# Gate tables of two expert blocks written by accumulating indirect DMAs in place of one-hot products

## The chip, the core and the metric

The kernel runs on one core of a Trainium2 chip. The metric is the device time of one execution in microseconds, from the first to the last instruction of the program with what little lies around it. The engines are named as the profile names them: PE (TensorE: matrix products, and PEld its weight loads), DVE (VectorE), ACT (ScalarE), POOL (GpSimd, which here only issues indirect DMAs), SP (SyncE, which issues every other DMA). Each engine works through its own instructions strictly in order; the engines wait for each other and for DMAs through semaphores.

## What is computed

One decoder layer on 1024 tokens of width 1024, all in float32: an attention branch and an mLSTM branch, merged by gates (the "front" below), and then a PEER expert layer on the result. The expert layer is the part that the change touches. Cut to what matters:

```python
q = (xb @ w_query).reshape(t, 8, 2, 64)                     # 8 heads, 2 halves
s = einsum('thpd,hpkd->thpk', q, sub_keys)                  # 128 keys for each half
top_s, top_i = top_k(s, 16)
cand_s = top_s[:, :, 0, :, None] + top_s[:, :, 1, None, :]  # 16 x 16 pairs
best_s, best_pos = top_k(cand_s, 16)                        # 16 experts of 16384, for each head
gate = softmax(best_s)
act = gelu(einsum('td,thkd->thk', xb, expert_down[idx]))
out = einsum('thk,thkd->td', gate * act, expert_up[idx])
```

So each token has 8 x 16 = 128 chosen experts, each with a gate. An expert's number is a pair (i, j) of two key numbers below 128. Two heads of a token may choose the same expert; its gates then add.

## The kernel before

The 1024 tokens are 8 blocks of 128, in 4 groups of two blocks. `front` runs once for each group: projections (`wpart` loads a piece of a weight strip, L209; for most strips it is split into a high part `whi` by ACT, L214, and a low part `wlo` by DVE, L215, and PE multiplies three times, L231 to L233; the later strips are multiplied unsplit, L229), attention, mLSTM, merging, the query product, and the scores `sc`, which go to HBM.

The expert layer is done in two ways. Blocks 0, 6 and 7 are "sparse": `down` gathers, for each of the 128 choices, one row of 4 KB for each token from HBM by an indirect DMA on POOL (`fetch`, L743), and DVE forms the product of that row with the token (L756, a product with a sum, followed by a short read of the sum); `up` gathers the second table in the same way and accumulates (L770). Blocks 1 to 5 are "dense": `dense` runs over all 16384 experts, 128 at a time in `hidden` (L809: PE products; then ACT's gelu and DVE's product with the gates, L816) and sums in `outputs` (L830 to L834). For this a dense block's gates are needed as a full table [expert][token], mostly zeros, in HBM (`gate_d`).

`topk` (DVE for the most part) finds the choices of a block while the next group's front runs. For a dense block, `spread` then makes the table by one-hot products: for each token DVE builds two matrices, `oi` (row i holds the gate, L727) and `oj` (column j holds a one, L730, a fourth of them on ACT), and PE multiplies them (L735), which puts each gate into the cell (i, j) and adds where two fall into one. Four tokens are a "quad": 4 products, one copy by ACT into `stage` (L736); four quads fill one `stage` of 1 MB, which SP writes to `gate_d` (L738). A dense block has 32 quads, five blocks have 160. The front asks for them by `fill`, 3 quads for 4 calls, within the gate and output projections of the following group: block 1 in group 1's front, blocks 2 and 3 in group 2's, blocks 4 and 5 in group 3's.

Block 0's `down` is done during the front. Its 128 products each stand behind one matmul of the front (`pace`: a dependence without a semaphore, on places from 0.4 to 0.95 of the front's list of matmuls), and its gathers use two buffers `g` (pool `gather`): gather n can be issued when product n-2 is done. Blocks 6 and 7's `down` and the `up` of all three run during `dense`, with five buffers.

The order of instructions on each engine is set by the Tile scheduler, from priorities (as a rule the order in which the code is written; `later` puts the `topk` of a group 5000 steps later) and from its own estimate of when operands are ready. Indirect DMAs of POOL share eight semaphores, so each waits for the one eight before it.

Of the kernel before, what the change touches and what calls it, by code (L numbers as in the profile page):

```python
# [10 lines left out]

F32 = mybir.dt.float32
F32R = mybir.dt.float32r
I32 = mybir.dt.int32
U32 = mybir.dt.uint32
AF = mybir.ActivationFunctionType
ALU = mybir.AluOpType
AX = mybir.AxisListType
PSUM = bass.MemoryType.PSUM
NOSYNC = mybir.DependencyInfo(mybir.DependencyClass.NoSync, mybir.DependencyReason.DATA)  # L20

P = 128
S = 1024
# [10 lines left out]
TMAX = P * max(len(g) for g in GROUPS)  # L34
SPARSE = (0, 6, 7)
DENSE = (1, 2, 3, 4, 5)
ND = P * len(DENSE)
GT = 16
GJ = 4
EG = 4  # L40
LATER = 5000
QUADS = 0.75
PACE0, PACE1 = 0.4, 0.95
WB = 4
PD0, PD1 = 0.06, 0.98

# [8 lines left out]
def layout(inputs):  # L55
    w = np.asarray(inputs["w_in"])[0]
    cols = [w[:, :1024], w[:, 1280:3328], w[:, 3344:6416],
            np.asarray(inputs["w_branch_attn"])[0], np.asarray(inputs["w_branch_mlstm"])[0],
            np.asarray(inputs["w_out"])[0], np.asarray(inputs["peer_w_query"])[0],
            w[:, 1024:1280]]  # L60
    a = {}
    a["x"] = np.asarray(inputs["x"])[0]
    a["pos"] = np.asarray(inputs["positions"])[0].reshape(NB, P).T
    a["wmain"] = np.concatenate([strips(c) for c in cols], axis=0)
    a["wif"] = w[:, 3328:3344].reshape(NC, P, 16).transpose(1, 0, 2)
    col = lambda v: np.asarray(v)[0].reshape(NC, P).T
# [18 lines left out]
    a["iota"] = np.arange(P, dtype=np.float32)[None]  # L85
    return {k: np.ascontiguousarray(v) for k, v in a.items()}


def build(nc, tc, a, out, dbg=None):
# [5 lines left out]
    dp = pool("dram", 1, outer, space=bass.MemoryType.DRAM)  # L95
    kp = pool("topk", 2)
    ks = pool("spread", 1)
    gp = pool("gather", 2)
    st = pool("state", 1)
    wp = pool("weights", 1)  # L100
    fp = pool("front", 1)
# [29 lines left out]
    gains = const("gains", [P, 3, NC], pool=st)  # L131
    x_first = []
    pos = const("pos", [P, NB], dt=I32, pool=st)
    freq = bcast("freq", 8, st)
    qkg = bcast("qkg", 128, st)
    wifr = t4([P, NC, 16], "wifr")
# [54 lines left out]
    xb_d = dp.tile([NB, P, D], F32, name="xb_d")  # L191
    xbT_d = dp.tile([len(DENSE), P, NC, P], F32, name="xbT_d")
    sc_d = dp.tile([NB, 2, P, 8, P], F32, name="sc_d")
    gate_d = dp.tile([P, P // GJ, ND // GT, GJ, GT], F32, name="gate_d")

    RING = 3
    kT = st.tile([P, 2, RING, P], F32, name="kT")
# [9 lines left out]
    def wpart(i, q, split):  # L207
        t = wp.tile([P, 4, 256], F32, name="w", bufs=WB)
        SY.dma_start(t, a["wmain"][i, :, 4 * q:4 * q + 4, :])  # L209
        if not split:  # L210
            return t, None
        hi = wp.tile([P, 4, 256], F32R, name="whi", bufs=3)
        lo = wp.tile([P, 4, 256], F32R, name="wlo", bufs=3)
        A.copy(hi, t)  # L214
        V.tensor_tensor(lo, t, hi.bitcast(F32), ALU.subtract)  # L215
        return hi, lo
# [430 lines left out]
    def topk(b):  # L647
# [15 lines left out]
        for qh in range(4):  # L663
# [23 lines left out]
            for p, n in ((0, 17), (1, 16)):  # L687
# [4 lines left out]
                V.tensor_tensor(eqh, eqh, tif[:, :, p, None, 0:n].to_broadcast([P, 2, 16, n]), ALU.mult)  # L692
                V.tensor_reduce(ef[:, p, cols], eq, AX.X, ALU.add)
        gate = (bp.tile([P, 8, 16], F32, name="gate", bufs=len(SPARSE)) if b in SPARSE
                else ks.tile([P, 8, 16], F32, name="dgate", bufs=2))
# [7 lines left out]
        if b in SPARSE or dbg:  # L703
# [1 line left out]
            V.scalar_tensor_tensor(idx, ef[:, 1], 128.0, ef[:, 0], ALU.mult, ALU.add)  # L705
            probe("idx", idx, b)
            probe("gate", gate, b)
        if b in DENSE:
            r["spread"] = spread(ef, gate, DENSE.index(b))
        return r  # L710

    def spread(ef, gate, k):
# [3 lines left out]
            T.transpose(ps[:, n, :], src, ident)  # L716
        A.copy(cols, ps[:, 0:3, :])
        for c in range(P // GT):
            stage = ks.tile([P, P, GT], F32, name="stage", bufs=2)
            for q in range(GT // 4):  # L720
                ps = pat.tile([P, 4, P], F32, name="at")
                for u in range(2):
# [15 lines left out]
                    SY.dma_start(gate_d[:, :, k * (P // GT) + c], stage.rearrange("p (n g) t -> p n g t", g=GJ))  # L738
                yield

    def fetch(p, table, idx, s):
        t = p.tile([P, D], F32, name="g")
        G.indirect_dma_start(out=t, out_offset=None, in_=a[table],  # L743
                             in_offset=bass.IndirectOffsetOnAxis(ap=idx[:, s:s + 1], axis=0))
        return t

    def down(r, b, pace, p):
        act = bp.tile([P, P], F32, name="act", bufs=1)
        xb = bp.tile([P, D], F32, name="xb", bufs=1)
        SY.dma_start(xb, xb_d[b])  # L750
        gain = p.tile([P, D], F32, name="g")
        SY.dma_start(gain, a["gain2"].to_broadcast([P, D]))
        V.tensor_tensor(xb, xb, gain, ALU.mult)
        for s in range(P):
            t = fetch(p, "down", r["idx"], s)
            ins = V.tensor_tensor_reduce(out=t, in0=t, in1=xb, scale=1.0, scalar=0.0, op0=ALU.mult,  # L756
                                         op1=ALU.add, accum_out=act[:, s:s + 1])
            after(ins, next(pace, None))
        coef = bp.tile([P, P], F32, name="coef")
        A.activation(coef, act, AF.Gelu)  # L760
        V.tensor_tensor(coef, coef, r["gate"].rearrange("p h k -> p (h k)"), ALU.mult)
        r["coef"] = coef

    def up(r, b, pace, p):
        acc = p.tile([P, D], F32, name="acc", bufs=1)
# [8 lines left out]
    def dense():  # L774
# [26 lines left out]
        def hidden(j, g):  # L801
# [10 lines left out]
                    mark("dense", ins)  # L812
            act = tp.tile([P, ND], F32, name="act", bufs=1)
            A.activation(act.rearrange("p (u t) -> p u t", u=NH), ps[:, :, 0:W], AF.Gelu)
            av_ = act.rearrange("p (c t) -> p c t", t=GT)
            V.tensor_tensor(av_, av_, g, ALU.mult)  # L816
# [20 lines left out]

        work = []
        for n in range(P // EG):
            g = tp.tile([P, ND // GT, GJ, GT], F32, name="g")  # L840
            SY.dma_start(g, gate_d[:, n])
            new = []
            for e in range(EG):
                new.append(hidden(EG * n + e, g[:, :, e, :]))
# [19 lines left out]
    res = {}  # L864
# [14 lines left out]
            pass  # L879
    later(GROUPS[-1])  # L880
    names = anchors["front"]
    names = names[int(PACE0 * len(names)):int(PACE1 * len(names))]
    pace = iter([names[i * len(names) // P] for i in range(P)])
    down(res[0], 0, pace, gp)
    inner.close()
    gd = dense()
    names = anchors["dense"]
# [19 lines left out]
```

## Time and profile before

| | us |
|---|---|
| median of 3 timed runs | 3559.62 (3559.30 to 3559.77) |
| the profiled execution | 3545.12 |
| its span, first to last instruction | 3543.4 |
| first product of `dense` (L809) | 1734.9 |
| first and last one-hot product (L735) | 593.4, 1682.8 |
| first and last product of block 0's `down` | 646, 1599 |

The span has two parts: the front with everything that runs beside it (up to 1734.9 us), and `dense` (1734.9 us to the end). The groups' fronts begin to load anew at about 14, 366, 775 and 1249 us (every fiftieth `wlo`). "Busy" of an engine is time in which it has an instruction; "idle before" stands with what ended the idle time. The granted clock is TensorE's share of full speed.

### The profile page before, as it was taken

The numbers are of one execution on the slowest core, as the hardware profiler recorded it, in microseconds if no ns is written. First come the engines' busy times: TensorE is split into PE (matmuls) and PEld (weight loads), VectorE is DVE, ScalarE is ACT, GpSimd is POOL, SyncE is SP. The second block draws the span as 40 slices with busy tenths as digits, with TensorE's granted clock in tenths as the row PEclk, the third lists the DMA queues.
The fourth block names the chain that finished last, engine by engine and source line by source line (L and its number), as shares of the span: only waits on it lengthen the run. The fifth ranks groups of instructions, "written<-read, shape, count | busy, mean of one in ns | idle before, by whom it ended". The sixth has DMA issues, their size and how long they took to land.

```text
span 3543.4 us, 55473 instructions
## 1 busy us (share of the span) xinstructions
PE 3378.6 (95%) x20579; PEld 3044.3 (86%) x20579; DVE 2743.1 (77%) x6406; ACT 1363.0 (38%) x2730; POOL 985.7 (28%) x772
## 2 busy tenths in 40 slices
PE   7999999999998789989799999999999999999999
PEld 7898988888887678887688898999989999898998
DVE  5332689739898468988598988888888888889985
ACT  6652567338574346635322222222222222222221
POOL 0000000110001221110004654545455455545542
PEclk9999999999999888999899999999999999999999
DMA  4344434874378874686727988889888888888884
GB/s 149 108 143 166 164 115 145 256 261 141 117 212 252 274 247 150 206 244 174 252 101 276 329 307 321 321 284 329 285 315 305 294 321 299 312 308 302 325 288 160
DMA packets 386670, 846.66 MB, mean 239 GB/s; under 512 B 189280, under 2 KB 195168, under 8 KB 382304
## 3 DMA queue, kind: packets, MB, share of 16 engines
q1 hardware_dynamic: 275808, 440.42, 37.7%
q0 software_dynamic: 110592, 402.70, 32.5%
q8 instruction: 162, 2.65, 0.3%
q14 instruction: 108, 0.88, 0.1%
HBM read 780.11 MB, written 62.91 MB: 238 GB/s over the span
## 4 chain that ended last, share of the span: by engine, by line
PE 66%; DVE 13%; issue 8%; DMA 7%; POOL 3%; ACT 3%; SPq 0%; POOLq 0%; DVEq 0%; ACTq 0%
PE ph L809 19%; PE pj L229 8%; PE po L830 6%; PE po L833 6%; PE po L834 6%; PE pj L231 4%; PE pj L233 4%; PE pj L232 4%; DMA g<-down,idx 3%; POOL g L743 3%; DVE oi L727 2%; PE at L735 2%; DMA w<-wmain 1%; DVE g L756 1%; DMA g<-up,idx 1%
## 5 line engine op out<-in xcount | busy, mean ns | idle before, releaser
L743 POOL DMA_INDIRECT g<-down,idx x384 | 480.2, 1250 | 1769.3 <-DVE act L756 879.2
L743 POOL DMA_INDIRECT g<-up,idx x384 | 505.3, 1316 | 732.8 <-DVE acc L770 373.9
L756 DVE CUSTOM_DVE_ANT_0 g<-g,xb 128x1024 f32<-128x1024 f32 x384 | 462.6, 1219 | 167.2 <-DMA g<-down,idx 166.6
L770 DVE SCALAR_TENSOR_TENSOR acc<-g,coef,acc 128x1024 f32<-128x1024 f32 x384 | 491.7, 1281 | 46.8 <-DMA g<-up,idx 36.8
L830 PE MATMUL po<-hu,ah 128*128 128x512 f32 x1280 | 499.2, 390 | 2.3 <-DVE y L836 2.3
L809 PE MATMUL ph<-xbh,hd 128*128 128x320 f32 x2048 | 470.6, 311 | 31.7 <-ACT hd L797 22.8
L833 PE MATMUL po<-lu,ah 128*128 128x512 f32 x1280 | 498.5, 389 | 0.0
L834 PE MATMUL po<-hu,al 128*128 128x512 f32 x1280 | 498.1, 389 | 0.0
L809 PE MATMUL ph<-xbh,ld 128*128 128x320 f32 x2048 | 470.5, 311 | 5.3 <-DVE ld L798 5.3
L809 PE MATMUL ph<-xbl,hd 128*128 128x320 f32 x2048 | 469.9, 311 | 0.0
L797 ACT CAST hu<-rawu 128x1024 fp32r<-128x1024 f32 x128 | 131.5, 1051 | 738.9 <-PE po L834 557.0
L809 PEld LDWEIGHTS ph<-xbh,hd 128*128 128x128 f32 x2048 | 346.6, 189 | 35.3 <-ACT hd L797 23.2
L215 DVE TENSOR_TENSOR wlo<-w,whi 128x1024 fp32r<-128x1024 f32 x200 | 243.3, 1218 | 142.1 <-ACT whi L214 142.0
L809 PEld LDWEIGHTS ph<-xbh,ld 128*128 128x128 f32 x2048 | 345.1, 189 | 7.0 <-DVE ld L798 6.7
L809 PEld LDWEIGHTS ph<-xbl,hd 128*128 128x128 f32 x2048 | 345.6, 189 | 0.0
L214 ACT CAST whi<-w 128x1024 fp32r<-128x1024 f32 x200 | 209.3, 1047 | 235.9 <-DMA w<-wmain 100.1
L836 DVE TENSOR_TENSOR y<-po,y 128x512 f32<-128x512 f32 x320 | 218.2, 685 | 89.0 <-PE po L834 88.5
L830 PEld LDWEIGHTS po<-hu,ah 128*128 128x128 f32 x1280 | 240.3, 188 | 53.9 <-DVE y L836 4.7
L834 PEld LDWEIGHTS po<-hu,al 128*128 128x128 f32 x1280 | 240.3, 188 | 50.5 <-DVE al L820 0.3
L833 PEld LDWEIGHTS po<-lu,ah 128*128 128x128 f32 x1280 | 240.3, 188 | 48.5
L232 PE MATMUL pj<-wlo,hT 128*128 128x256 f32 x832 | 244.9, 295 | 23.9 <-DVE wlo L215 23.9
L231 PE MATMUL pj<-whi,hT 128*128 128x256 f32 x832 | 245.9, 296 | 1.1 <-ACT whi L214 1.1
(266 smaller groups left out, 6670.2 us busy)
## 6 DMA issues: line engine op xcount, KB each, us to landing
w<-wmain SPq DMA_DIRECT2D x328, 512.0 KB
rawd<-downT SPq DMA_DIRECT2D x128, 512.0 KB
rawu<-up SPq DMA_DIRECT2D x128, 512.0 KB
gate_d<-stage SPq DMA_DIRECT2D x40, 1024.0 KB
g<-gate_d SPq DMA_DIRECT2D x32, 1280.0 KB
x<-x SPq DMA_DIRECT2D x16, 512.0 KB
sc_d<-sc SPq DMA_DIRECT2D x16, 512.0 KB
sc<-sc_d SPq DMA_DIRECT2D x32, 256.0 KB
```

What stands on the lines that cost most here:

```text
L215: V.tensor_tensor(lo, t, hi.bitcast(F32), ALU.subtract)
L229: ins = T.matmul(ps, lh(c), rh(c), start=first, stop=last)
L231: T.matmul(ps, lh(c), rh(c), start=first, stop=False)
L232: T.matmul(ps, lh(c), rl(c), start=False, stop=False)
L743: G.indirect_dma_start(out=t, out_offset=None, in_=a[table], in_offset=bass.IndirectOffsetOnAxis(ap=idx[:, s:s + 1], axis=0))
L756: ins = V.tensor_tensor_reduce(out=t, in0=t, in1=xb, scale=1.0, scalar=0.0, op0=ALU.mult, op1=ALU.add, accum_out=act[:, s:s + 1])
L770: ins = V.scalar_tensor_tensor(acc, t, g, acc, ALU.mult, ALU.add)
L809: ins = T.matmul(ps[:, u, 0:W], w[:, c, :], x[:, c, u * W:u * W + W], start=first, stop=last)
L830: first = T.matmul(o, ah[:, tok], uh[:, cols], start=(e == 0), stop=False)
L833: T.matmul(o, ah[:, tok], ul[:, cols], start=False, stop=False)
L834: ins = T.matmul(o, al[:, tok], uh[:, cols], start=False, stop=(e == EG - 1))
L836: V.tensor_tensor(y[:, k, cols], o, y[:, k, cols], ALU.add)
```

## The change

Blocks 1 and 2 no longer use one-hot products. Their tables are `cells1` and `cells2` in HBM, set to zero at the start and then added to. `topk` computes for each choice the number of its cell (seven DVE instructions), and `scatter` issues 128 indirect DMAs for each block: each adds 128 gates (one for each token, 4 bytes each) to 128 cells. Within a head the 16 DMAs go to different cells; the first of a head waits until all 16 of the head before have landed (`SYNC`). The scatters are hung behind block 0's gathers: block 1's 128 behind gathers 24 to 61, block 2's 128 behind gathers 66 to 123. `down` of block 0 is now put at the highest priority, begins at 0.32 of the front's matmuls, and has three gather buffers. Blocks 3 to 5 are spread as before, with one `stage` buffer in place of two. The zeros are written by SP, 128 DMAs of 128 KB, one asked for behind each of the first 128 weight loads. `dense` loads the gates of its five blocks from three places and multiplies in two instructions.

```diff
+ADDED = (1, 2)
+SPREAD = (3, 4, 5)
+NA = len(ADDED)
+BESIDE = {1: (24, 62), 2: (66, 124)}
+ZP = 64
-PACE0, PACE1 = 0.4, 0.95
+PACE0, PACE1 = 0.32, 0.95
...
-    gp = pool("gather", 2)
+    gp = pool("gather", 3)
...
-    gate_d = dp.tile([P, P // GJ, ND // GT, GJ, GT], F32, name="gate_d")
+    gate_d = dp.tile([P, P // GJ, len(SPREAD) * P // GT, GJ, GT], F32, name="gate_d")
+    cells = {b: dp.tile([P // EG, P, EG, P], F32, name=f"cells{b}") for b in ADDED}
+    flat = {b: t.rearrange("n i e t -> (n i e t)") for b, t in cells.items()}
+    none = st.tile([P, P * P // ZP], F32, name="none")
+    V.memset(none, 0.0)
+    clear = iter([flat[b].rearrange("(z p f) -> z p f", z=ZP, p=P)[z] for b in ADDED for z in range(ZP)])
...
         SY.dma_start(t, a["wmain"][i, :, 4 * q:4 * q + 4, :])
+        for z in [next(clear, None)]:
+            if z is not None:
+                SY.dma_start(z, none)
...
-        if b in DENSE:
-            r["spread"] = spread(ef, gate, DENSE.index(b))
+        if b in ADDED:
+            r["cell"] = cell = ks.tile([P, P], I32, name="cell", bufs=NA)
...
+            V.tensor_scalar(cell, pf[:, 0], float(P), tokc, ALU.mult, ALU.add)
+        if b in SPREAD:
+            r["spread"] = spread(ef, gate, SPREAD.index(b))
...
-            stage = ks.tile([P, P, GT], F32, name="stage", bufs=2)
+            stage = ks.tile([P, P, GT], F32, name="stage", bufs=1)
...
+    def scatter(b, pace):
+
+        cell, vals = res[b]["cell"], res[b]["gate"].rearrange("p h k -> p (h k)")
+        views = bass_types.dram_disjoint_views(flat[b][:, None], 16)
+        done = []
+        for h in range(8):
+            new = []
+            for s in range(16):
+                c = 16 * h + s
+                ins = G.indirect_dma_start(out=views[s], out_offset=bass.IndirectOffsetOnAxis(ap=cell[:, c:c + 1], axis=0),
+                                           in_=vals[:, c:c + 1], in_offset=None, compute_op=ALU.add)
+                if s == 0:
+                    for d in done:
+                        tc.add_manual_dep(ins.ins, d, SYNC, reason="heads")
+                else:
+                    after(ins, new[0])
+                after(ins, next(pace, None))
+                new.append(ins.ins.name)
+            done = new
...
-            av_ = act.rearrange("p (c t) -> p c t", t=GT)
-            V.tensor_tensor(av_, av_, g, ALU.mult)
+            a1_ = act[:, 0:NA * P].rearrange("p (k t) -> p k t", t=P)
+            a2_ = act[:, NA * P:].rearrange("p (c t) -> p c t", t=GT)
+            V.tensor_tensor(a1_, a1_, g[0], ALU.mult)
+            V.tensor_tensor(a2_, a2_, g[1], ALU.mult)
...
-    pace = iter([names[i * len(names) // P] for i in range(P)])
-    down(res[0], 0, pace, gp)
+    with tc.high_priority():
+        down(res[0], 0, paced(PACE0, PACE1), gp)
+    for b, (lo, hi) in BESIDE.items():
+        scatter(b, iter([fetched[lo + i * (hi - lo) // P] for i in range(P)]))
```

How instructions move is seen on POOL first. Before, its whole program after the start is gathers (L743), 128 of block 0's `down` first:

```order
L898 MEMSET const-uint8-127 128x1
L903 UNCONDITIONAL_BRANCH
L743 DMA g<-down,idx 128x1024 x128
L743 DMA g<-up,idx 128x1024 x128
L743 DMA g<-down,idx 128x1024 x256
L743 DMA g<-up,idx 128x1024 x256
```

Now, on the same engine, from the start (L773 is the gather, L804 the scatter into `cells`):

```order
L964 UNCONDITIONAL_BRANCH
L773 DMA g<-down,idx 128x1024 x25
L804 DMA cells_155<-dgate,cell 2097152x1 x4
L773 DMA g<-down,idx 128x1024
L804 DMA cells_155<-dgate,cell 2097152x1 x3
```

and where block 1's scatters end and block 2's begin:

```order
L804 DMA cells_155<-dgate,cell 2097152x1 x3
L773 DMA g<-down,idx 128x1024 x5
L804 DMA cells_156<-dgate,cell 2097152x1 x3
L773 DMA g<-down,idx 128x1024
L804 DMA cells_156<-dgate,cell 2097152x1 x2
```

Three or four scatters stand between two gathers for block 1, two or three for block 2; four gathers of `down` follow the last scatter, then `up`.

On DVE the place is the end of group 2's front, between the 150th and the 151st `wlo` (the part whose weights aren't split). Before, 37 of the 128 products stand there, one beside almost every quad, and 14 of them in one row at its end; a piece of it (L602 and L603 merge the branches, L756 is the product, L727 a one-hot matrix):

```order
L602 TENSOR_TENSOR gs<-pj,gs 128x256
L756 ISA g,act<-g,xb 128x1024
L756 ISA act 128x1
L603 TENSOR_TENSOR mixT<-mixT,gs 128x256
L756 ISA g,act<-g,xb 128x1024
L756 ISA act 128x1
L727 TENSOR_SCALAR oi<-iota,cols 128x128
```

Now 14 products stand between the same two `wlo`, most of them 20 to 30 instructions apart; a piece (L619 and L620 are the merging, L294 the next group's input, L755 and L758 the one-hot matrices):

```order
L758 TENSOR_SCALAR oj<-iota,cols 128x128
L619 TENSOR_TENSOR gs<-pj,gs 128x256 x2
L620 TENSOR_TENSOR mixT<-mixT,gs 128x256 x2
L294 SCALAR_TENSOR_TENSOR hTlow<-tp,gains,hT 128x128 x2
L755 TENSOR_SCALAR oi<-iota,cols 128x128
```

The products that left this place stand earlier: 37 of them up to the 100th `wlo`, where 24 stood before, and 37 between the 101st and the 149th, where 14 stood. From the 151st on there are 40, where there were 53.

On SP the order of the first group's DMAs changes. Before, after the start it holds weight loads (L209) and the next inputs (L298, L609):

```order
L209 DMA w<-wmain 128x1024 x32
L298 DMA x<-x 128x1024 x2
L209 DMA w<-wmain 128x1024 x13
L609 DMA x<-x 128x1024 x2
L209 DMA w<-wmain 128x1024 x28
```

Now the zeros (L226) stand among the first 30 weight loads (L223), single ones at first and later up to 13 in a row:

```order
L223 DMA w<-wmain 128x1024
L226 DMA cells_155<-none 128x256 x13
L223 DMA w<-wmain 128x1024 x2
L226 DMA cells_155<-none 128x256 x5
L223 DMA w<-wmain 128x1024
```

Behind those 30 the queue reads as before.

More of the change, by code (lines that the diff above doesn't have):

```diff
@@ L8 @@
 import concourse.tile as tile
+from concourse import bass_types
 from concourse import mybir
@@ L20 @@
 NOSYNC = mybir.DependencyInfo(mybir.DependencyClass.NoSync, mybir.DependencyReason.DATA)
+SYNC = mybir.DependencyInfo(mybir.DependencyClass.Sync, mybir.DependencyReason.DATA)
 P = 128
@@ L85, in layout @@
     a["iota"] = np.arange(P, dtype=np.float32)[None]
+    a["tokc"] = np.arange(P, dtype=np.float32)[:, None]
     return {k: np.ascontiguousarray(v) for k, v in a.items()}
@@ L133, in build @@
     pos = const("pos", [P, NB], dt=I32, pool=st)
+    tokc = const("tokc", [P, 1], pool=st)
     freq = bcast("freq", 8, st)
@@ L694, in topk @@
         gate = (bp.tile([P, 8, 16], F32, name="gate", bufs=len(SPARSE)) if b in SPARSE
-                else ks.tile([P, 8, 16], F32, name="dgate", bufs=2))
+                else ks.tile([P, 8, 16], F32, name="dgate", bufs=2 + NA))
         V.tensor_tensor(gate, bv, bv[:, :, 0:1].to_broadcast([P, 8, 16]), ALU.subtract)
@@ L707, in topk @@
             probe("gate", gate, b)
-        if b in DENSE:
-            r["spread"] = spread(ef, gate, DENSE.index(b))
+        if b in ADDED:
+            r["cell"] = cell = ks.tile([P, P], I32, name="cell", bufs=NA)
+            part = kp.tile([P, 2, P], I32, name="part", tag="eq", bufs=1)
+            pf = kp.tile([P, 2, P], F32, name="partf", tag="sc")
+            V.tensor_copy(part[:, 0], ef[:, 1])
+            V.tensor_single_scalar(part[:, 1], part[:, 0], EG - 1, ALU.bitwise_and)
+            V.tensor_single_scalar(part[:, 0], part[:, 0], 2, ALU.logical_shift_right)
+            V.tensor_copy(pf, part)
+            V.scalar_tensor_tensor(pf[:, 0], pf[:, 0], float(P), ef[:, 0], ALU.mult, ALU.add)
+            V.scalar_tensor_tensor(pf[:, 0], pf[:, 0], float(EG), pf[:, 1], ALU.mult, ALU.add)
+            V.tensor_scalar(cell, pf[:, 0], float(P), tokc, ALU.mult, ALU.add)
+        if b in SPREAD:
+            r["spread"] = spread(ef, gate, SPREAD.index(b))
         return r
@@ L739, in spread @@
                 yield
+    fetched = []
     def fetch(p, table, idx, s):
         t = p.tile([P, D], F32, name="g")
-        G.indirect_dma_start(out=t, out_offset=None, in_=a[table],
-                             in_offset=bass.IndirectOffsetOnAxis(ap=idx[:, s:s + 1], axis=0))
+        ins = G.indirect_dma_start(out=t, out_offset=None, in_=a[table],
+                                   in_offset=bass.IndirectOffsetOnAxis(ap=idx[:, s:s + 1], axis=0))
+        fetched.append(ins.ins.name)
         return t
@@ L839, in dense @@
         for n in range(P // EG):
-            g = tp.tile([P, ND // GT, GJ, GT], F32, name="g")
-            SY.dma_start(g, gate_d[:, n])
+            ga = tp.tile([P, NA, EG, P], F32, name="ga")
+            gs = tp.tile([P, len(SPREAD) * P // GT, GJ, GT], F32, name="g")
+            for k, b in enumerate(ADDED):
+                SY.dma_start(ga[:, k], cells[b][n])
+            SY.dma_start(gs, gate_d[:, n])
             new = []
             for e in range(EG):
-                new.append(hidden(EG * n + e, g[:, :, e, :]))
+                new.append(hidden(EG * n + e, (ga[:, :, e, :], gs[:, :, e, :])))
                 if n == 0 and e == 0:
@@ L881, in build, with paced @@
     names = anchors["front"]
-    names = names[int(PACE0 * len(names)):int(PACE1 * len(names))]
-    pace = iter([names[i * len(names) // P] for i in range(P)])
-    down(res[0], 0, pace, gp)
+    def paced(lo, hi):
+        return iter([names[int((lo + i * (hi - lo) / P) * len(names))] for i in range(P)])
+    with tc.high_priority():
+        down(res[0], 0, paced(PACE0, PACE1), gp)
+    for b, (lo, hi) in BESIDE.items():
+        scatter(b, iter([fetched[lo + i * (hi - lo) // P] for i in range(P)]))
     inner.close()
```

## The prediction

> **What bounds the kernel now.** I read the page first, then the busy time of each engine in stretches of the run, then the waits and the chain of the worst stretch, and last the groups of the lines that the change removes.
>
> ```profile
> span 3543.4 us, 55473 instructions
> PE 3378.6 (95%) x20579; PEld 3044.3 (86%) x20579; DVE 2743.1 (77%) x6406; ACT 1363.0 (38%) x2730; POOL 985.7 (28%) x772
> ```
>
> PE is the bound on average. The stretches (columns: stretch and its length; busy time of PE, PEld, DVE, ACT, POOL with counts; granted clock, DMA share, GB/s) say where it isn't:
>
> ```profile
> 14.00:365.00 351.00, 335.91 (x2228) 300.16 (x2230) 133.18 (x350) 175.85 (x406) 0.00 (x0) 0.96 0.41 139
> 640.00:800.00 160.00, 146.68 (x865) 132.62 (x865) 74.43 (x145) 49.82 (x98) 30.75 (x28) 0.96 0.83 273
> 1030.00:1310.00 280.00, 229.13 (x1395) 209.84 (x1394) 190.48 (x522) 112.85 (x244) 65.65 (x60) 0.88 0.86 269
> 1450.00:1600.00 150.00, 137.22 (x845) 121.67 (x844) 133.28 (x506) 72.35 (x178) 17.79 (x17) 0.95 0.74 211
> 1600.00:1715.00 115.00, 107.28 (x613) 92.76 (x611) 70.03 (x297) 58.50 (x144) 0.00 (x0) 0.97 0.66 177
> 1735.00:3543.00 1808.00, 1785.77 (x9984) 1629.65 (x9984) 1541.51 (x2147) 445.28 (x547) 843.09 (x640) 0.99 0.81 289
> ```
>
> The last row is `dense`: PE busy 99% at full clock. Nothing in the change takes PE work from it, so the time can come only from the front. The first row is a group without spreads and gathers: PE idle 15.1 of 351 us, 4.3%. The third is the worst: 50.9 of 280 us idle, clock 0.88. Who was waited for there (in all, times, longest; the 125.1 is the same wait over the whole front, 0 to 1660 us), what the chain consists of in its middle (1100 to 1180 us), and two of its pieces (start, us):
>
> ```profile
> POOL g L743 <- DVE act L756: 151.6, 39, 19.5
> DVE g L756 <- DMA g<-down,idx: 84.9, 34, 5.8
> ...
> DVE g L756 <- DMA g<-down,idx: 125.1, 49, 5.8
> ...
> PE pj L232 <- DVE wlo L215: 23.0, 4, 10.5
> by line: DMA g<-down,idx 44.6%; issue 18.8%; PE pj L229 10.3%; DVE g L756 9.6%; DVE oi L727 7.5%; POOL g L743 5.0%; PE at L735 4.6%; DVE oj L730 3.0%; PE tp L269 2.3%; DVE hTlow L277 1.5%; ACT hT L275 1.5%; ACT stage L736 0.6%; ACT oj L733
> 1113.57 6.42 DMA g<-down,idx
> 1148.96 7.65 DMA g<-down,idx
> ```
>
> It is a ring: POOL waits for a product to free one of two buffers, the gather lands 6.4 to 7.7 us after its issue, and DVE stands for 84.9 us with everything queued behind the product, one-hot matrices and `wlo` among it, for which PE waits. Two buffers let a product pass every 3.2 to 3.8 us at best, and the order has 37 of them in this place.
>
> **The change part by part.** The sum is made against the profiled execution, 3545.12 us; the timed runs have a median of 3559.62, 14.5 us more, and I put the differences onto that.
>
> *A. One-hot products of blocks 1 and 2 go.* 64 of 160 quads:
>
> ```profile
> L735 PE MATMUL at<-oj,oi 128*128 128x128 f32 x1280 | 201.6, 290 | 23.1 <-DVE oj L730 13.1 <-DVE oi L727 5.0 <-ACT oj L733 4.8
> L727 DVE TENSOR_SCALAR oi<-iota,cols 128x128 f32<-128x128 f32 x640 | 203.3, 342 | 9.8 <-PE at L735 6.8 <-ACT cols L717 2.9
> L730 DVE TENSOR_SCALAR oj<-iota,cols 128x128 f32<-128x128 f32 x480 | 133.7, 280 | 0.0
> 602.46 2.15 PE at L735 x16
> ```
>
> PE: 0.4 x 201.6 = 80.6 us, on the path since PE is the bound where they stand. Bounds: 512 matmuls at the 2.15/16 us of an unhindered run of them give 69; with the idle time before them, 0.4 x 23.1 = 9.2 more, 90. I take 81, since the busy time is what PE gets back. DVE's 0.4 x (203.3 + 133.7) = 135 us go too, and cover the seven instructions for each block's cell numbers.
>
> *B. The ring loosens.* Three buffers, and 14 products in place of 37 between the two `wlo` that frame the stall. At the 4.3% idle of the first group, 12 us of the 50.9 would remain: 39 us. The clock would be 0.96 in place of 0.88: 229 x (1 - 0.88/0.96) = 19 us. At most 58, at least 0; I take 40, about two thirds, since 37 products in place of 14 now stand between the 101st and the 149th `wlo`.
>
> *C. POOL gets 256 scatters between the gathers.* No row shows an accumulating DMA. What a gather costs POOL (in the stalled stretch; over all, min/median/max; one of the long ones), and the mean of SP's packets:
>
> ```profile
> L743 POOL DMA_INDIRECT g<-down,idx x60 | 65.6, 1094 | 260.4 <-DVE act L756 151.6 <-DVE oi L727 93.2 <-DVE oj L730 6.0
> L743 POOL DMA_INDIRECT g<-down,idx x384: 935/997/1992, 500.7 to 2839.1; - x192
> 1240.18 1.68 POOL g L743
> q1 hardware_dynamic: 275808, 440.42, 37.7%
> ```
>
> Issue: I take 1.09 us, the gather's, as the index list is as long. Each head waits for the head before to land: 16 waits of at most 6.4 us, the landing of a gather with a thousand times the bytes, over 256 scatters 0.4 us. So 1.5 us for each scatter. The engines' part: q1's packets took 0.377 x 16 x 3543 / 275808 = 77 ns on average; 8 reads and 8 writes for each of 16 engines are 1.2 us, below 1.5. What POOL has: the products hang on 0.32 to 0.95 of a front of some 1640 us (1735 less the sum below), so 1033 us for 128, 8.1 us each. Block 1 has 38 gathers, 307 us: (307 - 38 x 1.09) / 128 = 2.07 us for each scatter. Block 2 has 58, 468 us: 3.16. At 1.5 POOL keeps up on average. It won't where products stand close: 1.09 + 3.4 x 1.5 = 6.2 us from product to product, and 14 stand in the end of group 1. The row 640 to 800, with as many gathers at 5 to 6 us each, had 13.3 us PE idle. I take +10 us (0 to 25); behind a late gather wait a DVE product, `wlo` and the merging, and PE for these. The last scatter stands ahead of four gathers, so the tables are ready before the products end, and `dense` waits for nothing new.
>
> *D. One `stage` buffer.* ACT's first copy of the next four quads now waits until SP's write has landed. SP's issue of it, and the nearest landing, a write of half the size:
>
> ```profile
> L738 SPq DMA_DIRECT2D gate_d<-stage x40: 512/518/675, 599.6 to 1683.7; - x40
> 1714.79 3.39 DMA sc_d<-sc
> ```
>
> Twice 3.39 and the issue are 7.3 us; a quad takes 265/64 = 4.1 us in the last group (1450 to 1715 us), so the copy is 3.2 us late, 24 times: 77 us at most. PE has three buffers `at` and can run two quads, 8.2 us, ahead of a late copy, so most of it is covered; I take half a microsecond each, +12, nearer to that cover.
>
> *E. Zeros.* 128 writes among the first 30 weight loads, up to 13 in one row. SP's issue and ACT's wait for weights in the first group:
>
> ```profile
> L209 SPq DMA_DIRECT2D w<-wmain x328: 327/328/9477, 6.9 to 1693.5; - x164
> ACT whi L214 <- DMA w<-wmain: 22.8, 7, 6.8
> ```
>
> 13 issues are 4.3 us, within the lead of four weight buffers; all 128 are 42, the upper end if nothing hid them. I take +3, and count in it the load of `gain` for block 0, which the priority puts ahead of all inputs.
>
> *F. `dense`.* The same bytes of gates in 96 loads, and a second product:
>
> ```profile
> L816 DVE TENSOR_TENSOR act<-act,g 128x640 f32<-128x640 f32 x128 | 104.7, 818 | 6.0 <-ACT act L814 6.0
> L602 DVE TENSOR_TENSOR gs<-pj,gs 128x256 f32<-128x256 f32 x32 | 13.4, 419 | 39.1 <-PE pj L229 39.0
> ```
>
> From 256 to 640 elements it grows by 399 ns, so the fixed part is 419 - 266 = 153 ns; 128 times it is 20 us on DVE, which has 1808 - 1541 = 267 us free there. Nothing for PE; if DVE were full, it would be those 20 us.
>
> Sum: -81 - 40 + 10 + 12 + 3 = -96 us. 3559.6 - 96 = 3464; the profiled execution 3449.
>
> **A rule weighed.** Issues on POOL come in two lengths, about 0.94 and 1.68 us, as rows above show. The Trainium skill ("SBUF — State Buffer", section "SBUF: two separate sides") says that GpSimd can't write DMA descriptors while DVE runs an operation that takes both ports of a pair. It speaks against this change, since one-hot work and POOL's issues run side by side. The trace shows the two lengths and no cause for them. As a mechanism from rows: all issues beside DVE's work take 1.68 us, a scatter 2.08 with its share of the head's wait, so block 1 needs 128 x 2.08 + 38 x 1.68 = 330 us of 307, and the front loses 23 us: 3487.
>
> **The rivals.**
> - Long issues, as just worked out: 3487. For: long issues occur, and the mean of 1094 ns is above the median. Against: the median is 997 ns, so most are short.
> - Late scatters: an accumulate costs POOL between 2.07 and 2.87 us with its waits, the gathers behind it come late in block 1's part, and DVE stands as it does now. At 2.47: 128 x 0.4 = 51 us lost, 3515. For: it reads before it writes, and every cell is a packet of its own. Against: eight may be in flight, and 77 ns a packet.
> - Slower than before: the same place from a price of 2.07 + 103/128 = 2.87 us on, where the loss in block 1's part has eaten the 96 us and the 7 of the measurement. At 3.5 us: 128 x 1.43 + 128 x 0.34 = 227 us, 3691. For: nothing in this trace bounds a read, an add and a write to HBM. Against: it needs more than three times the gather's median issue.
> - The spreads stay slow: the late copy into the single `stage` isn't covered, 77 in place of 12 us: 3529.
> - More is won: the stall goes wholly and C and D are hidden: -81 - 58 + 3, 3424.
>
> **How the numbers follow.** Forecast 57 in 100, long issues 10, late scatters 12, slower 11, `stage` 5, more 5. Predicted 3464. From 3420 to 3540 all but the slower case and part of the late one lie, so about 85 in 100; if the sum holds, 3430 to 3500. What a measurement can tell from no change is some 0.2%, 7 us: faster 0.87, same 0.02 (the far end of late scatters), slower 0.11.
>
> **What would show it.** A: 768 rows of the one-hot product, about 121 us. B: DVE's wait for `g<-down` in the front well below 125 us in all, PE idle under 10% in the worst stretch, clock above 0.93. C: POOL's scatter rows near 1.1 us, POOL waiting for products and not products for POOL; `dense` beginning near 1640 us. D: ACT's waits before the copy into `stage` short and none on PE. E: first `wlo` as early as now within some us. F: `dense` 1808 us long as before. Wrong it would be by a scatter over 2 us, seen as DVE waiting for `g<-down` behind scatters, or by a `dense` that grows.

## The result, and the profile after

The changed kernel takes 3470.79 us (median of 4 runs, 3461.28 to 3474.27), the kernel before 3559.46 beside it: a ratio of 0.9752, interval 0.9727 to 0.9777. Forecast were 3464 us. The time is right to 7 us, but not the sum: two of its terms are off by some 40 us each, in opposite directions, and that they cancel is luck, as the experiments show.

The page of the changed kernel, and its groups for the adding DMA (busy, mean ns of one, idle before them), the one-hot product, the copy into `stage` and the two products with the gates; the last line has the shortest, median and longest adding DMA in ns:

```profile
span 3459.5 us, 54381 instructions
PE 3309.9 (96%) x20061; PEld 2980.2 (86%) x20061; DVE 2655.4 (77%) x6101; ACT 1289.8 (37%) x2535; POOL 1414.7 (41%) x1028
...
L804 POOL DMA_INDIRECT cells<-dgate,cell x256 | 442.8, 1730 | 115.0 <-issue 76.5 <-DMA cells<-dgate,cell 37.6 <-DMA g<-down,idx 0.6
L763 PE MATMUL at<-oj,oi 128*128 128x128 f32 x768 | 118.7, 285 | 3.4 <-ACT stage L764 1.9 <-ACT oj L761 0.9 <-DVE oj L758 0.4
L869 DVE TENSOR_TENSOR act<-act,g 128x384 f32<-128x384 f32 x128 | 71.5, 558 | 0.0
L868 DVE TENSOR_TENSOR act<-act,ga 128x256 f32<-128x256 f32 x128 | 53.5, 418 | 6.0 <-ACT act L865 6.0
L764 ACT COPY stage<-at 128x512 f32<-128x512 f32 x96 | 52.1, 592 | 44.5 <-DMA gate_d<-stage 24.0 <-PE at L763 20.2
...
L804 POOL DMA_INDIRECT cells<-dgate,cell x256: 1542/1565/3239, 645.5 to 1470.0; - x128
```

Its stretches, with the columns of those shown of before; the last row is the whole front, from 14 us to the first product of `dense`:

```profile
14.00:371.00 357.00, 341.48 (x2236) 304.52 (x2237) 133.32 (x350) 177.70 (x411) 0.00 (x0) 0.94 0.57 183
640.00:860.00 220.00, 180.42 (x1106) 162.04 (x1104) 107.26 (x292) 79.29 (x176) 172.75 (x112) 0.89 0.74 195
1000.00:1330.00 330.00, 312.76 (x2099) 277.74 (x2099) 256.78 (x883) 183.43 (x436) 211.50 (x132) 0.95 0.81 223
14.00:1650.20 1636.20, 1522.83 (x10077) 1351.25 (x10077) 1100.64 (x3810) 840.06 (x1982) 597.82 (x384) 0.93 0.68 197
```

The same two of before, the stretch that held its stall and the whole front:

```profile
1000.00:1330.00 330.00, 277.90 (x1755) 254.34 (x1755) 240.06 (x719) 150.16 (x339) 67.40 (x61) 0.90 0.83 252
14.00:1734.90 1720.90, 1592.74 (x10595) 1414.59 (x10595) 1197.20 (x4233) 911.62 (x2173) 142.39 (x128) 0.94 0.60 187
```

The stall of before is nearly gone: PE idle 17.2 of 330 us, 52.1 before. A new one stands at 640 to 860 us: PE idle 39.6 of 220 us at a clock of 0.89, where POOL is busy for 172.75 us. Who is waited for there:

```profile
DVE g L787 <- DMA g<-down,idx: 86.8, 17, 10.0
...
POOL cells L804 <- issue: 22.6, 72, 0.9
POOL cells L804 <- DMA cells<-dgate,cell: 12.8, 12, 4.0
POOL g L773 <- DVE act L787: 11.7, 4, 10.8
```

The products of block 0 wait for their gathers again, and now POOL hardly waits for products: of its 11.7 us, 10.8 stand ahead of the gather at 643.5 us, before the first adding DMA. Its instructions of L773 (gathers) and of L804 (adding DMAs) alone, in that stretch:

```profile
640.00:860.00 220.00, 30.31 (x26) 0.89 0.74 195
640.00:860.00 220.00, 142.44 (x86) 0.89 0.74 195
```

Over the run an adding DMA takes POOL (442.8 + 115.0) / 256 = 2.18 us with what stands ahead of it: 1.73 busy, 0.30 of "issue" and 0.15 of waiting for an earlier one to land. In this stretch the adding DMAs take 142.44 us and 22.6 + 12.8 ahead of them, the 26 gathers 30.31 and some 0.3 ahead of each: 216 of the 220 us are full, with a gather every 8.5 us.

### The profile page after: what moved, and what is told of

Its sections match the earlier page's. It is cut to its first block, busy times and chain, and to the rows that moved or that the text cites. A ratio compares the mean times of both kernels' runs of the same rounds, so it can differ in the third digit from the quotient of the medians.

```text
span 3459.5 us, 54381 instructions
## 1 busy us (share of the span) xinstructions
PE 3309.9 (96%) x20061; PEld 2980.2 (86%) x20061; DVE 2655.4 (77%) x6101; ACT 1289.8 (37%) x2535; POOL 1414.7 (41%) x1028
## 2 busy tenths in 40 slices
DMA packets 385531, 846.77 MB, mean 245 GB/s; under 512 B 163568, under 2 KB 185840, under 8 KB 385264
## 4 chain that ended last, share of the span: by engine, by line
PE 55%; DVE 11%; DMA 5%; issue 3%; POOL 2%; ACT 1%; DVEq 0%; POOLq 0%; SPq 0%; ACTq 0%
PE ph L860 20%; PE po L883 7%; PE po L887 7%; PE po L886 7%; PE pj L246 4%; PE pj L248 2%; PE pj L250 2%; PE pj L249 2%; PE at L763 2%; DVE g L787 1%; DMA w<-wmain 1%; POOL g L773 1%; DMA g<-up,idx 1%; DMA rawu<-up 1%; DVE oi L755 1%
## 5 line engine op out<-in xcount | busy, mean ns | idle before, releaser
L773 POOL DMA_INDIRECT g<-down,idx x384 | 480.6, 1252 | 1118.9 <-DVE sc L674 506.4
L773 POOL DMA_INDIRECT g<-up,idx x384 | 491.1, 1279 | 755.3 <-DVE acc L821 396.6
L804 POOL DMA_INDIRECT cells<-dgate,cell x256 | 442.8, 1730 | 115.0 <-issue 76.5
```

What stands on the lines that cost most here:

```text
L773: ins = G.indirect_dma_start(out=t, out_offset=None, in_=a[table], in_offset=bass.IndirectOffsetOnAxis(ap=idx[:, s:s + 1], axis=0))
L804: ins = G.indirect_dma_start(out=views[s], out_offset=bass.IndirectOffsetOnAxis(ap=cell[:, c:c + 1], axis=0), in_=vals[:, c:c + 1], in_off ...
```

## The experiments

Theory 1: the sum's parts stand, but each adding DMA costs POOL more than was forecast, and 3.4 of them to a gather make the gathers late. The rivals are that the idle comes from the priority of block 0's products, that the ring was loosened by the one-hot work that left and not by the order, and that it is the DMAs themselves (their number, their traffic) and not POOL's time. Ratios are to the kernel before on the same chip (medians of 3546 to 3554 us).

**The order alone.** All five dense blocks by one-hot products; of the change stay the buffers, the pace, the priority, the single `stage` (the edit is against the kernel before, and cut):

```diff
-PACE0, PACE1 = 0.4, 0.95
+PACE0, PACE1 = 0.32, 0.95
...
-    gp = pool("gather", 2)
+    gp = pool("gather", 3)
...
-            stage = ks.tile([P, P, GT], F32, name="stage", bufs=2)
+            stage = ks.tile([P, P, GT], F32, name="stage", bufs=1)
...
-    down(res[0], 0, pace, gp)
+    with tc.high_priority():
+        down(res[0], 0, paced(PACE0, PACE1), gp)
```

> The order alone: all five dense blocks get their gates by one-hot products, as before; of the change there remain the third gather buffer, the pace that begins at 0.32, the highest priority of block 0's products and the single stage buffer. No adding DMA, no clearing DMA, gates multiplied in one operation. Theory 1 (the parts add up: the products taken away are worth some 83 us, the looser ring some 45, the adding DMAs and the clearing cost some 35): 3500 to 3530 us, with PE idle below 25 us between 1000 and 1300. Rival (the ring was only loosened because the builds of the one-hot operands of two blocks left VectorE): 3545 to 3565 us, and block 0's products still wait over 80 us for their gathers. Rival (order and priority are worth nearly everything, and the gates of blocks 1 and 2 little): below 3490 us.

Measured: 3486.69 us, ratio 0.9814 (0.9795 to 0.9833), 13 us below theory 1's range and in that of the last rival; the next run refutes that rival's other half. Its stretches and the wait that was 125.1 us before:

```profile
14.00:371.00 357.00, 341.01 (x2262) 304.88 (x2262) 134.18 (x351) 178.06 (x412) 0.00 (x0) 0.96 0.41 138
1000.00:1330.00 330.00, 312.91 (x2072) 282.79 (x2071) 272.38 (x988) 185.93 (x452) 37.97 (x37) 0.92 0.76 226
14.00:1682.10 1668.10, 1578.68 (x10596) 1405.93 (x10596) 1194.84 (x4232) 908.92 (x2171) 140.88 (x128) 0.94 0.62 193
...
DVE g L756 <- DMA g<-down,idx: 4.7, 2, 3.1
...
ACT stage L736 <- DMA gate_d<-stage: 36.8, 17, 3.9
...
PE at L735 <- ACT stage L736: 5.8, 3, 3.2
```

With all one-hot work in place the ring's wait falls to 4.7 us and PE's idle time in the front from 128.2 to 89.4. So buffers, pace and priority by themselves heal the stall, and are worth 1.86%, 66 us. The single `stage` holds ACT for 36.8 us and PE for 5.8.

**No adding DMAs.** The cells are cleared and read, and nothing is added:

```diff
-    for b, (lo, hi) in BESIDE.items():
-        scatter(b, iter([fetched[lo + i * (hi - lo) // P] for i in range(P)]))
```

> The changed kernel with the 256 adding DMAs left out (the cells are cleared and read as before, so the gates of blocks 1 and 2 are zero). Theory 1 (the adding DMAs hold up block 0's gathers on GpSimd's queue, and this makes the 39.6 us of PE idle and the clock of 0.89 between 640 and 860 us): PE idle there falls to 10 to 15 us, the wait of block 0's products for their gathers from 86.8 us between 650 and 860 to below 15, and the time is 3425 to 3450 us. Rival (the idle is there because block 0's products at the highest priority are served ahead of the front's own work on VectorE, whatever GpSimd does): PE idle there stays above 30 us and the time at 3460 to 3475.

Measured: 3415.92 us, 0.9609 (0.9592 to 0.9626), on the chip of the last run. The two stretches (all that POOL does there is gathers):

```profile
640.00:860.00 220.00, 208.02 (x1437) 184.93 (x1435) 146.55 (x464) 115.46 (x280) 36.95 (x31) 0.98 0.66 220
14.00:1599.40 1585.40, 1498.57 (x10078) 1332.55 (x10078) 1096.70 (x3808) 840.60 (x1980) 147.40 (x128) 0.95 0.64 203
```

PE idles 12.0 us between 640 and 860 us, as theory 1 expected, and the time lies 9 us below its range. The priority isn't what makes the idle: it is there unchanged. What the front asks of POOL is to be seen too: 31 gathers in 220 us, one in 7.1 us. Over the whole of block 1's part, from the issue of gather 24 to that of gather 62, it is 281.6 us (636.0 to 917.6) for 38 gathers, 7.4 each; the changed kernel took 331.3 (643.5 to 974.8). Nor does the traffic of the adding DMAs make a gather late: between 640 and 860 us a gather landed 5.3 us after its issue in the median with them and 5.9 without, a weight load 4.6 and 4.9. It is the issue that comes late. Between this run and the order alone lie the one-hot products of two blocks, less the clearing: 2.05%, 73 us. Between it and the changed kernel lie the adding DMAs: 1.43%, 51 us. In the fronts it is 50.8: PE idle 26.5 us more, and busy 24.3 us longer for the same matmuls, at the lower clock. Block 1's part alone, at 331.3 against 281.6, accounts for 49.7. The changed kernel wasn't timed beside these kernels, and one program below differed by 54 us between two chips; so I lean on the waits and the places where the time is lost more than on the difference of the ratios.

**No priority.** The changed kernel without it:

```diff
-    with tc.high_priority():
-        down(res[0], 0, paced(PACE0, PACE1), gp)
+    down(res[0], 0, paced(PACE0, PACE1), gp)
```

> The changed kernel without the highest priority for block 0's products; three gather buffers, pace and adding DMAs stay. Theory 1 (a product that is served late holds its buffer, so the next gather and the adding DMAs behind it start late; the priority is a part of what loosened the ring): 3485 to 3530 us, and PE idle comes back somewhere between 900 and 1300. Rival (the third buffer and the earlier pace did it, the priority does nothing): within 8 us of the changed kernel, 3463 to 3479. Rival (the priority hurts, since it puts front work behind block 0's): 3440 to 3460.

Measured: 3522.75 us, 0.992 (0.9905 to 0.9934), within theory 1's range; without the priority most of the gain is lost.

```profile
1000.00:1330.00 330.00, 264.85 (x1697) 239.31 (x1696) 206.74 (x645) 140.33 (x320) 241.52 (x156) 0.90 0.78 212
...
DVE g L787 <- DMA g<-down,idx: 180.4, 47, 28.3
```

The stall of before is back at its old place, with 65 us of PE idle in 330 and 180.4 us of waits for gathers in the front (96.3 in the changed kernel).

**The wider spacing.** Fewer adding DMAs for each gather up to the 80th, more behind it:

```diff
-BESIDE = {1: (24, 62), 2: (66, 124)}
+BESIDE = {1: (24, 80), 2: (80, 124)}
```

> The changed kernel with the adding DMAs of block 1 hung between gathers 24 to 80 and those of block 2 between 80 and 124 (24 to 62 and 66 to 124 in the changed kernel): 2.3 for each gather instead of 3.4 where PE idles, 2.9 instead of 2.2 behind. Theory 1 (a gather's round of 1.0 + 0.3 + 3.4 x 1.86 = 7.6 us is what exceeds the pace between 640 and 860; with 2.3 it is 5.6): PE idle there falls from 39.6 to some 20 us and the time to 3448 to 3462 us. Rival (the stall only moves, to the stretch from 1000 on in which block 2's stand thicker): 3463 to 3480 us. Rival (the number for each gather does not matter, since it is not GpSimd that is late): 3465 to 3475 with PE idle above 30 us between 640 and 860.

Measured: 3429.41 us, 0.9656 (0.9639 to 0.9673), 19 us below theory 1's range. All other engines have the same instructions in the same order as in the changed kernel; only POOL's queue differs.

```profile
640.00:860.00 220.00, 207.00 (x1424) 184.61 (x1424) 143.76 (x460) 114.83 (x277) 158.75 (x101) 0.97 0.76 218
...
DVE g L787 <- DMA g<-down,idx: 27.8, 8, 6.0
...
640.00:860.00 220.00, 36.78 (x31) 0.97 0.76 218
640.00:860.00 220.00, 121.97 (x70) 0.97 0.76 218
```

Now 31 gathers get through, as with no adding DMAs, beside 70 adding ones (86 in the changed kernel): 70 x 2.18 + 31 x (36.78/31 + 0.3) = 199 of 220 us. PE's idle time falls to 13.0 us, the clock rises to 0.97, and gathers 24 to 62 take 287.5 us in place of 331.3. Most of the 51 us was a queue that asked for more time than it had.

**Thick at the end.** Block 1's as in the wider spacing, block 2's 128 closer:

```diff
-BESIDE = {1: (24, 62), 2: (66, 124)}
+BESIDE = {1: (24, 80), 2: (86, 124)}
```

> The version with the wider spacing for block 1 (gathers 24 to 80), and block 2's 128 adding DMAs squeezed between gathers 86 and 124: 3.4 for each gather, as block 1's had in the changed kernel, but at the end of the front instead of between 640 and 860 us. With no adding DMAs the products 84 to 124 of block 0 came 7.0 us apart (1181 to 1447 us), a gather's round with 3.4 of them takes 7.6. Theory 1 (the number for each gather decides, wherever it stands): block 0's products wait for their gathers between 1150 and 1500, PE idle there grows by 15 to 30 us, 3445 to 3470 us. Rival (the place decides: the end of group 1's front has no slack, the end of the whole front has some): within 8 us of the wider version, 3421 to 3438.

Measured: 3445.16 us, 0.9711 (0.9695 to 0.9727), inside theory 1's range. Between 1150 and 1500 us, first of this kernel, then of the wider spacing:

```profile
DVE g L787 <- DMA g<-down,idx: 24.1, 10, 4.8
1150.00:1500.00 350.00, 320.41 (x2222) 285.05 (x2220) 293.02 (x1055) 188.34 (x456) 243.21 (x149) 0.92 0.73 188
```

```profile
DVE g L787 <- DMA g<-down,idx: 9.7, 2, 6.8
1150.00:1500.00 350.00, 334.84 (x2323) 298.59 (x2321) 306.28 (x1104) 195.18 (x472) 225.39 (x134) 0.92 0.74 198
```

PE idles 29.6 us in place of 15.2. The number for each gather counts at this place too, by PE's idle time at about half the price: 14.4 us here, 26.6 between 640 and 860 us. The pace of 7.0 us in the expectation isn't what its trace shows: with no adding DMAs, gathers 86 to 124 are issued from 1100.9 to 1421.6 us, 8.4 us each. A round of one gather (some 1.5 us with what is ahead of it) and 3.37 adding DMAs at 2.18 is 8.8, so it exceeds the pace by 0.4 us here, and by 1.4 in block 1's part. That fits the lower price.

**Two gather buffers.** In the changed kernel:

```diff
-    gp = pool("gather", 3)
+    gp = pool("gather", 2)
```

> The changed kernel with two gather buffers instead of three; priority, pace and adding DMAs stay. Theory 1 (with two buffers a gather can be issued only when the product before last is done, and with 3.4 adding DMAs behind each gather GpSimd then waits for VectorE as well as VectorE for GpSimd): 3490 to 3540 us. Rival (GpSimd's own time for each round is what is late, and the priority serves each product at once, so two buffers are enough): within 8 us of the changed kernel, 3460 to 3478.

Measured: 3486.16 us, 0.9822 (0.9809 to 0.9835), a little below theory 1's range and outside the rival's. Over the front VectorE waits for gathers and POOL for products, by turns, and both longer than in the changed kernel (96.3 and 104.9 us):

```profile
DVE g L787 <- DMA g<-down,idx: 144.8, 36, 10.1
POOL g L773 <- DVE act L787: 136.5, 29, 16.7
```

**Evenly spread.** 2.56 for each gather:

```diff
-BESIDE = {1: (24, 62), 2: (66, 124)}
+BESIDE = {1: (24, 74), 2: (74, 124)}
```

> The changed kernel with the adding DMAs spread evenly, block 1's between gathers 24 and 74 and block 2's between 74 and 124: 2.56 for each gather throughout, a round of 1.3 + 2.56 x 1.86 = 6.1 us. Theory 1 (what counts is that a round stays below the pace of some 7.0 to 7.4 us): within 6 us of the wider version (2.3, then 2.9), 3422 to 3436. Rival (each adding DMA costs by itself in the stretch where it stands, and the stretch before 860 us is the dearer): 3437 to 3450. Rival (the last stretch, where the wider version still stands 2.9 thick, is the dearer): 3412 to 3421.

Measured: 3445.03 us, 0.9708 (0.9695 to 0.9722). This agrees with the first rival, that the stretch before 860 us is the dearer. Its profile doesn't bear that out: PE idles 14.4 us there, 13.0 in the wider spacing. The profiled executions are 7.4 us apart, and PE's idle time in their fronts 6 (99.6 and 93.5 us). The rest stays open, all the more for what the next kernel did on the same chip.

**Writing in place of adding.** The changed kernel, with

```diff
-                                           in_=vals[:, c:c + 1], in_offset=None, compute_op=ALU.add)
+                                           in_=vals[:, c:c + 1], in_offset=None)
```

> The changed kernel with indirect DMAs that write their gate instead of adding it (a cell that two heads of a token choose keeps one head's gate). Theory 1 (adding is what makes the DMA dear on GpSimd: 1.57 us against 1.01 of a gather): the row falls to 1.0 to 1.2 us, a round with 3.4 of them to about 5.6, and the time to 3425 to 3450 us. Rival (the price belongs to an indirect DMA whose indexed side is in device memory as single elements, adding or not): the row stays at 1.5 to 1.6 us and the time within 8 us of the changed kernel, 3460 to 3478.

Measured: 3475.36 us, 0.9782 (0.9762 to 0.9801). The DMA took POOL 0.963 us in the median, near theory 1's 1.0 to 1.2, and the time was the rival's. DVE's longest waits from 640 to 1000 us:

```profile
DVE wlo L232 <- ACT whi L231: 32.7, 9, 20.5
DVE g L787 <- DMA g<-down,idx: 13.9, 4, 6.9
DVE wlo L232 <- issue: 12.1, 5, 5.6
DVE x L631 <- issue: 11.7, 2, 10.7
DVE gs L619 <- remote: 10.0, 1, 10.0
DVE x L631 <- remote: 9.5, 2, 5.7
```

The last four, 43 us, name no cause, and the traces of the four kernels on this chip hold no landing times of DMAs. Three more kernels were made to tell whether plain writes are dear in themselves.

**Reads at the same places.** Each adding DMA becomes an indirect read of the same cells into a spare tile:

```diff
-                ins = G.indirect_dma_start(out=views[s], out_offset=bass.IndirectOffsetOnAxis(ap=cell[:, c:c + 1], axis=0),
-                                           in_=vals[:, c:c + 1], in_offset=None, compute_op=ALU.add)
+                ins = G.indirect_dma_start(out=back[:, c:c + 1], out_offset=None, in_=flat[b][:, None],
+                                           in_offset=bass.IndirectOffsetOnAxis(ap=cell[:, c:c + 1], axis=0))
```

> The changed kernel with each of the 256 adding DMAs replaced, at its place in GpSimd's queue, by an indirect DMA that reads the same 128 cells into a spare tile, one element for each partition (nothing is added, so the gates of blocks 1 and 2 stay zero). All other engines have the same instructions in the same order as in the changed kernel and in the one with plain writes. Theory 1 (what costs is GpSimd's time between the gathers; the plain writes bring a further cost of their own as writes): the row is 0.95 to 1.0 us, a round 5.6 us, and the time 3418 to 3440 us. Rival (it is the number of DMAs that stand ahead of a gather, not GpSimd's time for them; then plain writes are no exception): 3455 to 3480 us, as with plain writes.

Measured: 3414.62 us, 0.9623 (0.9601 to 0.9645), 3 us below theory 1's range and about as fast as with no DMAs there at all.

```profile
L804 POOL DMA_INDIRECT back<-cells,cell x256: 938/945/2855, 637.1 to 1433.7; - x128
...
640.00:860.00 220.00, 207.81 (x1394) 185.56 (x1393) 140.37 (x452) 112.88 (x272) 148.35 (x130) 0.95 0.65 212
```

3.4 DMAs ahead of a gather cost next to nothing if each holds POOL for 0.945 us in the median; gathers 24 to 62 take 289.2 us. So it isn't their number.

**Plain writes in the wider spacing.** Both edits, `BESIDE = {1: (24, 80), 2: (80, 124)}` and no `compute_op`:

> Indirect DMAs that write instead of adding (a cell that two heads of a token choose keeps one head's gate), in the wider spacing (gathers 24 to 80, 80 to 124). Only GpSimd's queue differs from the version with plain writes in the first spacing (3475 us). Theory 1 (plain writes carry a cost of their own, which no wait in the profile names, whatever their spacing): 3455 to 3480 us, no gain over the first spacing and well above the adding ones in the wider spacing (3429). Rival (spacing cures both alike): 3415 to 3435 us.

Measured: 3420.86 us, 0.9637 (0.9616 to 0.9659), as the rival had it.

**Plain writes again**, the same kernel on another chip:

> The kernel with plain writes in the first spacing once more, unchanged (a cell that two heads of a token choose keeps one head's gate), since it alone does not fit: reads of the same length at the same places gave 3415 us, plain writes in the wider spacing 3421. Theory 1 (GpSimd's time between the gathers is what costs, and the 3475 us had a cause outside the kernel's program): 3415 to 3440 us, and the waits without a named cause, 57 us on VectorE before, are gone. Rival (plain writes 3.4 to a gather have a cost of their own, which reads and thinner writes have not): 3460 to 3480 us again.

Measured: 3421.15 us, 0.9629 (0.9607 to 0.9652). Theory 1 holds:

```profile
L804 POOL DMA_INDIRECT cells<-dgate,cell x256: 954/963/3644, 635.1 to 1428.4; - x128
...
640.00:860.00 220.00, 207.37 (x1406) 184.40 (x1405) 141.75 (x455) 113.16 (x276) 151.35 (x131) 0.96 0.66 214
```

The waits without a name are gone; the two named ones above are 26.1 and 33.6 us. One program thus differed by 54 us between two chips, of which the kernel before shows nothing (3549.5 and 3554.3 us); why is open, and whether it is the chip at all. For the other three kernels of the first chip I therefore rely on the named waits and the idle time shown, not on differences of 16 us.

**Past the last gather.** The adding DMAs at 2.2 for each gather, the last 28 behind block 0's last gather:

```diff
-BESIDE = {1: (24, 62), 2: (66, 124)}
+BESIDE = {1: (24, 82), 2: (82, 140)}
...
-        scatter(b, iter([fetched[lo + i * (hi - lo) // P] for i in range(P)]))
+        scatter(b, iter([fetched[min(lo + i * (hi - lo) // P, P - 1)] for i in range(P)]))
```

> The adding DMAs at 2.2 for each gather throughout: block 1's between gathers 24 and 82, block 2's from 82 on, with the last 28 behind block 0's last gather, where GpSimd has nothing else to do until the dense stage. A round is 1.3 + 2.2 x 1.86 = 5.4 us everywhere. Theory 1 (the rounds must stay below the pace; the wider version's 2.9 for each gather in the last stretch still costs a part of the 13 us between it and the version with none): 3418 to 3427 us. Rival (what is left is the price of any spacing, the DMAs' traffic and the head waits): 3426 to 3434. Rival (the 28 behind the last gather make the dense stage wait for block 2's gates): above 3440.

Measured: 3420.21 us, 0.9644 (0.9619 to 0.9669), theory 1's range. It has the lowest median of the versions that do the whole computation, but the interval doesn't part it from the wider spacing. Its front:

```profile
14.00:1609.30 1595.30, 1509.29 (x10077) 1341.39 (x10078) 1100.68 (x3806) 839.36 (x1980) 601.05 (x384) 0.94 0.69 202
```

PE idles 86.0 us in it, 113.4 in the changed kernel and 86.8 with no adding DMAs.

## Why the prediction was right, and where it wasn't

- **A, one-hot products:** forecast 81 us. The group fell from 201.6 to 118.7, 82.9. The exchange by itself, from the order alone to no adding DMAs, took 80.1 us of PE's busy time. Right.
- **B, the ring:** right in mechanism, too small. Forecast were 40 us from B and 12 lost in D, 28 together; the order alone gave 66 (52.8 between the two profiled fronts). The step that failed is the third taken off B because more products stand together: their waits fell to 4.7 us all the same. Without it, 58 less the 5.8 that PE waits in D is 52, what the profiled fronts differ by. Most of the rest up to 66 lies between executions: the profiled one of before (3545.12 us) is among its fastest.
- **C, the adding DMAs:** forecast 10 us, measured 51. It is the term that failed, in two inputs. The price was taken as a gather's issue, 1.5 us with the head waits, and was 2.18: the issue itself 1.73 in place of 1.09, and 0.30 between two issues, which the sum left out. The pace was taken as an average of 8.1 us for each gather, 307 us for block 1's 38, and is 7.4, 281.6 us. At 2.18 and some 1.5 for a gather with what is ahead of it, 128 x 2.18 + 38 x 1.5 = 336 us of work, 54 more than the front leaves; measured were 331.3, 49.7 more. The place was named, and that a close stand of products could not be kept up with; it was priced far too low. This is the rival of late scatters. At 2.18 us its own sum would have given 128 x 0.11 = 14, since it used the same average pace. The prediction's own signs show it too, though the time was met: it named "a scatter over 2 us, seen as DVE waiting for `g<-down` behind scatters" as a sign of being wrong, and these are the 2.18 and the 86.8 us; and it wanted the worst stretch under 10% PE idle at a clock above 0.93, where 640 to 860 us has 18% and 0.89.
- **D, one `stage`:** forecast 12 us; PE waits 1.9 us for it here and 5.8 with all blocks one-hot, ACT 24.0 and 36.8. PE's lead over ACT covers nearly all.
- **E, zeros:** forecast 3. At 371 us PE is 26 matmuls behind the order alone, which would be 26 x 357 / 2262 = 4 us. But the wider spacing, with the same zeros, is not behind there (2262 matmuls), so no cost of the zeros is shown.
- **F, `dense`:** the two products take 418 + 558 = 976 ns where one took 818, a fixed part of 158 where 153 was estimated. From its first product to the end it is 1809.3 us, 1808.5 before. Right.
- **Long issues:** they exist, but don't make the price: the shortest adding DMA is 1542 ns and the median 1565, the mean 1730. Reads of 945 ns in the median have long ones as well. Of the Trainium skill's rule ("SBUF — State Buffer", section "SBUF: two separate sides") nothing more can be said: no run here changes what VectorE does beside them.

So the total was met by luck: the gain of B was 38 us too small (with D) and the loss of C 41 us too small. `dense` began at 1650 us, forecast near 1640.

## What to carry to other kernels

Price a queue by the stretch in which it is asked for most, not by its mean: add up what each round takes on its engine, waits included, and compare it with the pace that the other engines set; here block 1's gathers and adding DMAs took POOL 331 us where the front would have passed in 282, and PE idled 27.6 us more between 640 and 860 us. Where a table of numbers sets the places, thinning it out is the cheapest remedy: two numbers of `BESIDE` were worth another 1%. Measure each part of a change by itself, since two wrong terms can sum to the right time.

## What the runs showed of the hardware

Adding costs POOL more than writing: 1.565 us in the median against 0.963 for the same 128 elements written and 0.945 read. The packets show a difference as well, in the pages of no adding DMAs (with its queue of 768 gathers), of adding and of writing:

```profile
DMA packets 348665, 846.60 MB, mean 248 GB/s; under 512 B 126704, under 2 KB 148976, under 8 KB 348400
...
q0 software_dynamic: 110592, 402.70, 34.0%
```

```profile
DMA packets 385531, 846.77 MB, mean 245 GB/s; under 512 B 163568, under 2 KB 185840, under 8 KB 385264
```

```profile
DMA packets 356859, 846.77 MB, mean 248 GB/s; under 512 B 134896, under 2 KB 157168, under 8 KB 356592
```

That is (385531 - 348665) / 256 = 144 packets for an adding DMA and 32 for a writing one; a gather of 128 rows has 110592 / 768 = 144. The Trainium skill ("DMA: Bandwidth & Descriptors", section "Why a DMA increments its semaphore by 16 and not by 1") has all 16 engines post a completion for every DMA issued from GpSimd. By that, which agrees with the counts, 128 packets carry the added elements, one each, 16 the written ones and 128 the rows of a gather. Whether the packets make the price on POOL isn't shown: the gather has 144 too, at 1.0 us in the median.

The same matmuls don't take the same time: those of the front, 10,077 or 10,078 in the traces, kept PE busy for 1498.6 us at a granted clock of 0.95 (no adding DMAs, 86.8 us idle) and 1522.8 at 0.93 (the changed kernel, 113.4 us idle). Idle time alone doesn't set this: past the last gather it was 1509.3 us at 0.94 with 86.0 idle. So how much of the 24.3 us more comes from the longer idle time stays open.
